# Differential attention scores: stacked rounded-precision matmuls on 128 rows for full-precision matmuls on 64 rows

## The chip, the cores and the metric

The kernel runs on one core of a Trainium2 chip. The metric is the device time of one execution in microseconds (us). The core's engines each run their own queue of instructions in order: PE (TensorE, matmuls), DVE (VectorE), ACT (ScalarE), POOL (GpSimd) and SP (SyncE, which here only issues DMAs). They wait for each other by semaphores.

## The reference, cut to what matters

The reference is a network of six layers on 512 tokens of width 1024: pooling, gated delta rule, latent attention (MLA), pooling, a state-space layer and, last, a layer of differential attention. Only the last one is touched. Cut to its core:

```python
def odd_layer(x, positions, ...):
    q, k, v, gate = jnp.split(rmsnorm_2(x, norm_w) @ w_in, 4, axis=-1)
    q = rmsnorm_2(q.reshape(bsz, s, 8, 2, 64), q_norm_w)   # 8 heads, 2 maps of width 64
    k = rmsnorm_2(k.reshape(bsz, s, 8, 2, 64), k_norm_w)
    q, k = partial_rotary(q, positions), partial_rotary(k, positions)
    # for each block of 128 queries:
    sc = jnp.einsum("bqhmd,bkhmd->bhmqk", qblk, k) * 64 ** -0.5
    pr = softmax(where(allowed, sc, -inf))                 # block-causal, chunks of 64
    wts = pr[:, :, 0] - lam * pr[:, :, 1]
    o = einsum("bhqk,bkhe->bqhe", wts, v)
    o = rmsnorm_2(o, subln_w) * (1 - lam_init)
    return x + (o.reshape(...) * silu(gate)) @ w_out
```

All data is float32.

## The kernel before

Activations lie transposed: a tile holds 128 channels on the partitions and 512 tokens. Most matmuls avoid full precision by splitting an operand into a rounded part and the rest. `split` makes the two with a cast on ACT (to the type fp32r) and a subtraction on DVE; `load_w` does the same for each slab of weights that a DMA on SP brings (L275 the load, L278 the cast, L279 the rest). `mm3` (L285 to L287) then adds three rounded matmuls: high by high, high by low, low by high.

The last layer is `odd`. For each of eight heads there is a unit for the query (`query`), one for the key (`key`), one for the gate, and one for v per two heads. Each is a projection of 24 rounded matmuls per 512 columns (`proj`). The query unit scales the result (L1407), squares it for its norm (L353) and rotates it (`rope`: L970 to L973, four DVE instructions). The key unit sums the squares with a full-precision matmul against a constant (L1398, called the norm matmul below), forms 1/sqrt on ACT by Ln and Exp (L371, L373), applies it (L1400) and rotates. Both end in one tile of 128 partitions: map 0 of the head on partitions 0 to 63, map 1 on 64 to 127. The tiles have the tag `t`, a pool of 8 buffers.

`attend` works on one head. For each block of 128 queries (`qb`, 0 to 3) and each of the two maps it forms the scores with one full-precision matmul on the map's 64 partitions (L1462), 128 to 512 columns wide, masks (L1463), and calls `softmax_rows` (L993 to L997: maximum on DVE, exponential on ACT, reciprocal). The two maps are combined (L1466, L1467). `weighted` transposes the result (L1007), copies it (L1009) and multiplies with v (L1011). Sums of the squares over the head (L365) give the last norm.

```python
rs = slice(m * 64, m * 64 + 64)
ps = self.ps("a")
nc.tensor.matmul(ps[:, :n], q[rs, sl], k[rs, :n], start=True, stop=True)
```

In the program, `attends` is a generator that the loop at the end of `odd` steps through between the units, by a table of numbers (`steps`); a head starts once its key is there. The final order of each engine's instructions is set when the kernel is built: a scheduler moves instructions within what data and buffers allow, so PE's queue mixes projections of later heads with the attention of earlier ones. The chip then runs each queue in that fixed order.

`stacked` exists already; the latent attention uses it for its rotated queries: of 64 partitions it makes a tile of 128, the rounded part on one half and the rest on the other.

Of the kernel before, what the change touches and what calls it, by code (L numbers as in the profile page):

```python
# [10 lines left out]
F32 = mybir.dt.float32  # L11
F32R = mybir.dt.float32r
I32 = mybir.dt.int32
AF = mybir.ActivationFunctionType
ALU = mybir.AluOpType
# [155 lines left out]
def step(chain, n):  # L171
    for _ in range(n):
        next(chain, 0)


def weave(units, *chains, drain=True):

    for u in units:
        u()
        for chain, n in chains:  # L180
            step(chain, n)
    if drain:
        for chain, _ in chains:
            for _ in chain:
                pass
# [7 lines left out]
class Net:  # L193
# [782 lines left out]
    def stacked(self, src, tag):  # L976
# [9 lines left out]
            out.append(t)  # L986
        return out

    def softmax_rows(self, ps, n, scale):

        nc = self.nc
        st = self.small([P, 4], "smx", 8)
        nc.vector.tensor_reduce(st[:, 0:1], ps[:, :n], axis=AX.X, op=ALU.max, negate=True)  # L993
        nc.vector.tensor_scalar(st[:, 1:2], st[:, 0:1], scale, None, op0=ALU.mult)  # L994
        pr = self.big("c")
        nc.scalar.activation(pr[:, :n], ps[:, :n], AF.Exp, bias=st[:, 1:2], scale=scale, accum_out=st[:, 2:3])  # L996
        nc.vector.reciprocal(st[:, 3:4], st[:, 2:3])  # L997
        return pr, st[:, 3:4]
# [373 lines left out]
    def odd(self):  # L1372
        nc, a = self.nc, self.a
        r = self.norm_r()
        rn = self.tok_r(r)
        cos, sin = self.rope_tables("pos2", "drope")
        mask = list(range(8, 16)) + list(range(8)) + list(range(16, 32))
        l4 = self.big("c", shape=[P, 4, 64])
        nc.gpsimd.dma_start(l4.rearrange("p a b -> p (a b)"), a["l4"].to_broadcast([P, 256]))
        pr = self.big("c", shape=[P, 2, 64])  # L1380
        lm = self.small([P, 4], "lam", 1)
        for i in range(2):
            nc.vector.tensor_tensor(pr[:, i], l4[:, 2 * i], l4[:, 2 * i + 1], op=ALU.mult)
            nc.vector.tensor_reduce(lm[:, i : i + 1], pr[:, i], axis=AX.X, op=ALU.add)
        nc.scalar.activation(lm[:, 0:2], lm[:, 0:2], AF.Exp)
        self.log_exp()
        nc.vector.tensor_tensor(lm[:, 2:3], lm[:, 1:2], lm[:, 0:1], op=ALU.subtract)
        nc.vector.tensor_scalar(lm[:, 2:3], lm[:, 2:3], -LAM_INIT, None, op0=ALU.add)
        nlam = lm[:, 2:3]

        def key(m):
            (ps,) = self.proj([a["dif_in"][m]], self.h, 8)
            st = sts[m - 8]
            st["qs"] = query_scale(st["q"][1])
            t = self.scaled(ps, r)
            (_, sq) = self.sq_add(None, t)
            p2 = self.ps("b")
            nc.tensor.matmul(p2, self.c("b64"), sq, start=True, stop=True)  # L1398
            rr = self.rsqrt(p2, 1.0 / 64, EPS, tag="t")
            nc.vector.scalar_tensor_tensor(t, t, self.p("kn"), rr, op0=ALU.mult, op1=ALU.mult)  # L1400
            return self.rope(t, cos, sin, mask, "t")

        def query(m):

            (ps,) = self.proj([a["dif_in"][m]], self.h, 8)
            t = self.big("t")
            nc.scalar.mul(t, ps, self.p("qn"))  # L1407
            (_, sq) = self.sq_add(None, ps)
            return self.rope(t, cos, sin, mask, "t"), sq

        def query_scale(sq):
            pn = self.ps("b")[:, :8].rearrange("p (c n) -> p c n", c=4)
            self.tok_sums(sq, self.c("b64")[:, 0:P:64], pn)
            return self.tok_scale(pn, rn, 64, 64.0**-0.5, "qs2", 2)

        y, sts = [], [{} for _ in range(8)]

        def v(hd):
            vN = [self.big("y", shape=[P, 2, 256]) for _ in range(2)]
            self.projn(  # L1420
                [a["dif_v"][hd + i] for i in range(2)], self.h, 4, 256,
                lambda t, ps: nc.scalar.mul(vN[t // 2][:, t % 2], ps, rn[:, t : t + 1]),
            )
            sts[hd]["v"] = sts[hd + 1]["v"] = vN

        def q(hd):
            sts[hd]["q"] = query(hd)

        def k(hd):
            sts[hd]["k"] = key(8 + hd)  # L1430

        def gate(hd):
            (ps,) = self.proj([a["dif_in"][16 + hd]], self.h, 8)
            sts[hd]["z"] = (self.scaled(ps, r, "y"), self.last, {})
            if hd % 2:
                self.silus([sts[i]["z"] for i in (hd - 1, hd)])
                for i in (hd - 1, hd):
                    sts[i]["g"] = sts[i]["z"][0]
                gated()

        def gated():

            while len(y) < 8 and "t" in sts[len(y)] and "g" in sts[len(y)]:
                t, g = sts[len(y)]["t"], sts[len(y)]["g"]
                nc.vector.tensor_tensor(t, t, g, op=ALU.mult)
                y.append(self.split(t))

        def attend(hd, st):
            vN = st["v"]
            q, qs, k = st["q"][0], st["qs"], st["k"]  # L1450
            po = self.ps("c")
            vs = slice((hd % 2) * P, (hd % 2) * P + P)
            vh = [vN[t // 2][:, t % 2, vs] for t in range(NC)]
            prev = None
            for qb in range(NC):
                n = (qb + 1) * P
                sl = slice(qb * P, n)
                pm = []
                for m in range(2):
                    rs = slice(m * 64, m * 64 + 64)  # L1460
                    ps = self.ps("a")
                    nc.tensor.matmul(ps[:, :n], q[rs, sl], k[rs, :n], start=True, stop=True)  # L1462
                    nc.vector.memset(ps[0:64, n - 64 : n], NEG)  # L1463
                    pm.append(self.softmax_rows(ps, n, qs[:, qb, m : m + 1]))
                (p0, r0), (p1, r1) = pm
                nc.vector.tensor_scalar(p1[:, :n], p1[:, :n], r1, nlam, op0=ALU.mult, op1=ALU.mult)  # L1466
                nc.vector.scalar_tensor_tensor(p0[:, :n], p0[:, :n], r0, p1[:, :n], op0=ALU.mult, op1=ALU.add)  # L1467
                if prev is not None:
                    self.weighted(*prev)
                prev = (p0, qb, vh, po, "y")  # L1470
                yield 1
            self.weighted(*prev)
            yield 1
            ro = self.rsqrt(self.sq_sum(self.sq_add(None, po), "b"), 1.0 / P, EPS, mul=1.0 - LAM_INIT)
            st["t"] = self.big("y")
            nc.vector.scalar_tensor_tensor(st["t"], po, self.p("subln"), ro, op0=ALU.mult, op1=ALU.mult)
            gated()
            yield 1

        def attends():  # L1480
            for hd in range(8):
                while "k" not in sts[hd]:
                    yield 1
                yield from attend(hd, sts[hd])

        chain = attends()
        order = [(u, 2 * p + i) for p in range(4) for u, i in ((v, 0), (q, 0), (k, 0), (q, 1), (k, 1), (gate, 0), (gate, 1))]
        order = order[:19] + order[21:26] + order[19:21] + order[26:]
        steps = (2, 2, 2, 0, 2, 1, 3, 2, 2, 3, 1, 3, 2, 1, 2, 2, 2, 1, 2, 2, 2, 2, 2, 2, 2, 3, 2, 2)
        for (u, hd), n in zip(order, steps):  # L1490
            u(hd)
            step(chain, n)
        last = [self.load_w(a["dif_out2"], D)]

        def slabs(m):
            return [(a["dif_out"][m], 7, 0, P), (last[0], 1, m * P, D)]

        early, rest = self.out_units(slabs, y, None, ["mm"] * 3)
        weave(early, (chain, 4))
        for u in rest:  # L1500
            u()
# [48 lines left out]
```

## Time and profile before

| | |
|---|---|
| median of 3 runs | 2570.8 us (2565.99 to 2572.75) |
| the profiled execution | 2575.46 us, its span 2573.7 us |
| mean granted clock of PE | 0.983 |
| PE busy | 2476.2 us (96%) |
| weight loads (PEld) | 1976.5 us (77%) |
| DVE busy | 1628.0 us (63%) |
| ACT busy | 1062.2 us (41%) |
| POOL busy | 466.2 us (18%) |

Busy times are sums over the whole span. PE's weight loads run beside its matmuls. Matmuls are pipelined: a listed duration overlaps the next one, so what a matmul costs is read from the distance between starts. The median and the profiled execution are different runs of the same kernel. POOL has no work in the last layer but two loads near its start.

### The profile page before, as it was taken

What the parts mean: (1) busy time and instruction counts of PE and PEld (TensorE: products, weight loads), DVE (VectorE), ACT (ScalarE), POOL (GpSimd) and SP (SyncE); (2) the same over time, 40 slices, a digit from 0 to 9 for tenths busy, and PEclk for the clock granted to TensorE, in tenths of its full rate; (3) what the DMA queues carried; (4) which work ended last, traced back from release to release, by engine and by line L of the source; (5) the groups of instructions that cost most, each with busy time, mean ns of one, the idle gap of its engine ahead of it and who ended that gap; (6) DMA issues with size and microseconds to landing.
All of it is one profiled execution on the core that took longest, in us unless ns stands there. A gap on an engine that the chain in (4) does not pass through costs nothing. (4 is left out here: it accounts for less than half of the span.)

```text
span 2573.7 us, 30632 instructions
## 1 busy us (share of the span) xinstructions
PE 2476.2 (96%) x11692; PEld 1976.5 (77%) x11692; DVE 1628.0 (63%) x2874; ACT 1062.2 (41%) x1676; POOL 466.2 (18%) x374
## 2 busy tenths in 40 slices
PE   8999999688899999999999999999999999999999
PEld 6888877476777888887787888887777767877877
DVE  6675368678556454355557366744997888477774
ACT  4333354134335343444445332333235546365553
POOL 0121103222321110000000112203334443200000
PEclk9999999799999999999999999999999999999999
DMA  4323224311211232211111233232222211321122
GB/s 152 98 91 99 94 82 127 100 36 46 80 56 58 90 95 97 86 60 56 62 58 53 95 98 95 94 100 88 83 88 67 67 50 58 113 66 58 58 64 76
DMA packets 81907, 205.63 MB, mean 80 GB/s; under 512 B 28352, under 2 KB 28480, under 8 KB 81760
## 3 DMA queue, kind: packets, MB, share of 16 engines
q1 hardware_dynamic: 81264, 202.23, 24.7%
q8 instruction: 92, 1.51, 0.2%
q0 software_dynamic: 208, 0.66, 0.1%
q10 hardware_dynamic: 288, 0.79, 0.1%
q14 instruction: 55, 0.45, 0.1%
HBM read 196.30 MB, written 7.34 MB: 79 GB/s over the span
## 5 line engine op out<-in xcount | busy, mean ns | idle before, releaser
L285 PE MATMUL psmm<-h,wh 128*128 128x512 f32 x1704 | 691.1, 406 | 47.9 <-DVE t L552 32.0
L278 ACT CAST wh<-wr 128x1024 fp32r<-128x1024 f32 (+3 forms) x366 | 376.6, 1030 | 779.2 <-PE psmm L286 591.5
L286 PE MATMUL psmm<-h,wh 128*128 128x512 f32 x1704 | 686.5, 403 | 0.1
L287 PE MATMUL psmm<-h,wl 128*128 128x512 f32 x1704 | 684.1, 401 | 0.0
L279 DVE TENSOR_TENSOR wl<-wr,wh 128x1024 fp32r<-128x1024 f32 (+2 forms) x270 | 322.1, 1193 | 185.9 <-ACT wh L278 182.4
L285 PEld LDWEIGHTS psmm<-h,wh 128*128 128x128 f32 x1704 | 324.9, 191 | 129.6 <-issue 54.5
L287 PEld LDWEIGHTS psmm<-h,wl 128*128 128x128 f32 x1704 | 324.3, 190 | 81.8 <-issue 14.7
L285 PE MATMUL psmm<-y,wh 128*128 128x512 f32 x976 | 385.2, 395 | 0.0
L286 PE MATMUL psmm<-y,wh 128*128 128x512 f32 x976 | 384.5, 394 | 0.0
L287 PE MATMUL psmm<-y,wl 128*128 128x512 f32 x976 | 383.0, 392 | 0.0
L286 PEld LDWEIGHTS psmm<-h,wh 128*128 128x128 f32 x1704 | 324.8, 191 | 73.3 <-issue 7.7
L279 POOL TENSOR_TENSOR wl<-wr,wh 128x1024 fp32r<-128x1024 f32 (+1 forms) x96 | 237.7, 2478 | 532.6 <-ACT wh L278 410.2
L351 POOL TENSOR_TENSOR sq<-sq,sq 128x512 f32<-128x512 f32 x36 | 64.5, 1791 | 845.4 <-ACT sq L353 845.4
L285 PEld LDWEIGHTS psmm<-y,wh 128*128 128x128 f32 x976 | 183.4, 188 | 38.9 <-issue 1.6
L286 PEld LDWEIGHTS psmm<-y,wh 128*128 128x128 f32 x976 | 183.5, 188 | 37.9 <-issue 2.2
L287 PEld LDWEIGHTS psmm<-y,wl 128*128 128x128 f32 x976 | 183.4, 188 | 37.5 <-issue 0.5
L1175 DVE SCALAR_TENSOR_TENSOR psa<-y,par,psa 128x506 f32<-128x506 f32 (+28 forms) x232 | 164.9, 733 | 3.2 <-ACT psa L1171 0.9
L480 DVE TENSOR_TENSOR x<-psmm,x 128x512 f32<-128x512 f32 x44 | 30.4, 692 | 140.2 <-PE psmm L287 140.2
L996 ACT ACTIVATE c<-psa,smx,qs 128x128 f32<-128x128 f32 (+3 forms) x128 | 78.8, 616 | 88.1 <-DVE smx L994 87.5
L492 DVE TENSOR_TENSOR t<-psmm,r 128x512 f32<-128x512 f32 (+1 forms) x74 | 50.9, 688 | 100.8 <-PE psmm L287 100.7
L552 DVE SCALAR_TENSOR_TENSOR t<-psmm,par,t 128x511 f32<-128x511 f32 (+2 forms) x120 | 89.0, 743 | 7.3 <-ACT t L547 5.4
L257 ACT CAST y<-c 128x512 fp32r<-128x512 f32 x60 | 37.1, 620 | 90.3 <-POOL c L528 69.3
(362 smaller groups left out, 3343.0 us busy)
## 6 DMA issues: line engine op xcount, KB each, us to landing
wr<-in_pool_in_dram SPq DMA_DIRECT2D x64, 512.0 KB, 3.4
wr<-in_gdn_in_dram SPq DMA_DIRECT2D x48, 512.0 KB, 3.5
wr<-in_ssd_in_dram SPq DMA_DIRECT2D x48, 512.0 KB, 3.4
wr<-in_pool_out_dram SPq DMA_DIRECT2D x32, 512.0 KB, 3.4
wr<-in_mla_in_dram SPq DMA_DIRECT2D x27, 512.0 KB, 3.4
wr<-in_dif_in_dram SPq DMA_DIRECT2D x24, 512.0 KB, 3.5
wr<-in_mla_uq_dram SPq DMA_DIRECT2D x24, 384.0 KB, 3.0
wr<-in_pool_grp_dram SPq DMA_DIRECT2D x16, 512.0 KB, 3.4
```

The costliest lines, as they stand in the source:

```text
L257: nc.scalar.copy(hi, src)
L278: nc.scalar.copy(hi[:, :f], raw[:, :f])
L279: self.rest.tensor_tensor(lo[:, :f], raw[:, :f], hi[:, :f].bitcast(F32), op=ALU.subtract)
L285: nc.tensor.matmul(ps, wh, xh, start=start, stop=False)
L286: nc.tensor.matmul(ps, wh, xl, start=False, stop=False)
L287: nc.tensor.matmul(ps, wl, xh, start=False, stop=stop)
L351: (eng or nc.gpsimd).tensor_tensor(acc[0], acc[0], acc[1], op=ALU.add)
L480: self.nc.vector.tensor_tensor(self.x[m], ps, self.x[m], op=ALU.add)
L492: self.last = self.nc.vector.tensor_tensor(t[:n], ps[:n], r[:n], op=ALU.mult)
L552: self.last = nc.vector.scalar_tensor_tensor(t[:, s:], u[:, : S - s], w(k), t[:, s:], op0=ALU.mult, op1=ALU.add)
L996: nc.scalar.activation(pr[:, :n], ps[:, :n], AF.Exp, bias=st[:, 1:2], scale=scale, accum_out=st[:, 2:3])
L1175: nc.vector.scalar_tensor_tensor(out[:, s:], z[:, : S - s], dw(k), acc[:, s:], op0=ALU.mult, op1=ALU.add)
```

## The change

The scores become two rounded matmuls over 128 partitions. With q = qh + ql and k = kh + kl (rounded part and rest), a tile with qh on one half of the partitions and ql on the other, times kh on both halves, gives (qh + ql) kh; times kl on both halves, (qh + ql) kl. So for each map the query is stacked (`stacked`, once per head for both maps: two tiles with tag `t` beside the rotated one), and the key becomes four tiles with tag `y` (36 buffers): for each map the rounded part and the rest, each on both halves. The new function `stacked_twice` writes the map's own half with a cast on ACT and a subtraction on DVE and copies it to the other half with a DMA from SBUF to SBUF, issued by POOL, 64 partitions x 512 words each.

```diff
+    def stacked_twice(self, src, tag):
+
+        nc = self.nc
+        out = []
+        for i in range(2):
+            a, b = slice(i * 64, i * 64 + 64), slice(64 - i * 64, 128 - i * 64)
+            hi, lo = self.big(tag, F32R), self.big(tag, F32R)
+            nc.scalar.copy(hi[a], src[a])
+            nc.vector.tensor_tensor(lo[a], src[a], hi[a].bitcast(F32), op=ALU.subtract)
+            nc.gpsimd.dma_start(hi[b], hi[a])
+            nc.gpsimd.dma_start(lo[b], lo[a])
+            out.append((hi, lo))
         return out
...
-            return self.rope(t, cos, sin, mask, "t")
+            return self.stacked_twice(self.rope(t, cos, sin, mask, "t"), "y")
...
-            return self.rope(t, cos, sin, mask, "t"), sq
+            return self.stacked(self.rope(t, cos, sin, mask, "t"), "t"), sq
...
-                    rs = slice(m * 64, m * 64 + 64)
                     ps = self.ps("a")
-                    nc.tensor.matmul(ps[:, :n], q[rs, sl], k[rs, :n], start=True, stop=True)
+                    hi, lo = k[m]
+                    nc.tensor.matmul(ps[:, :n], q[m][:, sl], hi[:, :n], start=True, stop=False)
+                    nc.tensor.matmul(ps[:, :n], q[m][:, sl], lo[:, :n], start=False, stop=True)
```

The existing function that the query now calls:

```python
def stacked(self, src, tag):
    for i in range(2):
        a, b = slice(i * 64, i * 64 + 64), slice(64 - i * 64, 128 - i * 64)
        t = self.big(tag, F32R)
        nc.scalar.copy(t[a], src[a])
        nc.vector.tensor_tensor(t[b], src[a], t[a].bitcast(F32), op=ALU.subtract)
        out.append(t)
```

Lines after `stacked` stand 14 or 15 higher in the changed kernel (L1462 becomes L1476 and L1477, L1007 is L1021, L1011 is L1025, L1398 is L1412). The scheduler sets a new order in the whole layer. Three places follow, each before and then after.

PE at the first scores of the sixth head, before: the two maps' scores of the first block (psa) stand next to each other behind a sum of squares (L365).

```order
L285 MATMUL psmm_18607<-wh_18552,h_16738 128x256
L286 MATMUL psmm_18607<-wl_18553,h_16738 128x256
L287 MATMUL psmm_18607<-wh_18552,h_16739 128x256
L365 MATMUL psb_18660<-sq_18658,ones 128x512
L1462 MATMUL psa_18668<-t_18497,t_18406 128x128
L1462 MATMUL psa_18677<-t_18497,t_18406 128x128
L285 MATMUL psmm_18694<-h_16443,wh_18690 128x512
```

The same place after, from the last projection matmuls of the unit ahead of it; y_18636 and y_18637 are the first map's key (rounded part, rest), y_18642 and y_18643 the second's.

```order
L285 MATMUL psmm_18844<-h_16738,wh_18840 128x512
L286 MATMUL psmm_18844<-h_16739,wh_18840 128x512
L287 MATMUL psmm_18844<-h_16738,wl_18841 128x512
L1476 MATMUL psa_18816<-y_18636,t_18537 128x128
L1025 MATMUL psc_18446<-y_18674,y_18182 128x128 x2
L1025 MATMUL psc_18446<-y_18674,y_18183 128x128
L1021 MATMUL psb_18679<-con,c_18655 128x128 x4
L1477 MATMUL psa_18816<-y_18637,t_18537 128x128
L1476 MATMUL psa_18826<-y_18642,t_18540 128x128
L1477 MATMUL psa_18826<-y_18643,t_18540 128x128
```

Where two matmuls stood there are four, with other work between them. The norm matmul of this head's key stands 21 projection matmuls of 512 columns and three transposes ahead of the first one.

PE in the third head from the 512 column scores on, before: projection matmuls (psmm) stand between scores and transposes (L1007).

```order
L286 MATMUL psmm_17929<-h_16632,wh_17925 128x512
L1462 MATMUL psa_17789<-t_17670,t_17581 128x512
L1011 MATMUL psc_17675<-y_17744,y_17373 128x128 x2
L1462 MATMUL psa_17798<-t_17670,t_17581 128x512
L287 MATMUL psmm_17929<-h_16631,wl_17926 128x512
L285 MATMUL psmm_17929<-h_16669,wh_17925 128x512
L286 MATMUL psmm_17929<-h_16670,wh_17925 128x512
L287 MATMUL psmm_17929<-h_16669,wl_17926 128x512
L285 MATMUL psmm_17929<-h_16738,wh_17925 128x512
L286 MATMUL psmm_17929<-h_16739,wh_17925 128x512
L1007 MATMUL psb_17809<-con,c_17727 128x128 x3
```

The same head after, from its last 384 column scores to their transposes (L1021, x3).

```order
L1476 MATMUL psa_17805<-y_17739,t_17641 128x384
L1477 MATMUL psa_17805<-y_17740,t_17641 128x384
L1476 MATMUL psa_17871<-y_17733,t_17638 128x512
L1021 MATMUL psb_17817<-con,c_17775 128x128 x2
L1477 MATMUL psa_17871<-y_17734,t_17638 128x512
L1025 MATMUL psc_17745<-y_17820,y_17421 128x128 x2
L1476 MATMUL psa_17881<-y_17739,t_17641 128x512
L1477 MATMUL psa_17881<-y_17740,t_17641 128x512
L1021 MATMUL psb_17893<-con,c_17802 128x128 x3
```

No projection matmul stands there any more; between the scores and their transposes there are only this head's own matmuls.

POOL at the start of the last layer, before: its two loads of positions and constants are its last work.

```order
L351 TENSOR_TENSOR sq_16447<-sq_16447,sq_16598 128x512
L351 TENSOR_TENSOR sq_16447<-sq_16447,sq_16636 128x512
L351 TENSOR_TENSOR sq_16447<-sq_16447,sq_16674 128x512
L946 DMA c_16764<-in_pos_dram 128x512
L1379 DMA c_16791<-in_l_dram 128x256
```

After: behind them stand the copies of the key tiles, here those of the first head and the first two of the second.

```order
L946 DMA c_16764<-in_pos_dram 128x512
L1393 DMA c_16791<-in_l_dram 128x256
L998 DMA y_17030<-y_17030 64x512
L998 DMA y_17036<-y_17036 64x512
L999 DMA y_17031<-y_17031 64x512
L999 DMA y_17037<-y_17037 64x512
L998 DMA y_17203<-y_17203 64x512
L998 DMA y_17209<-y_17209 64x512
```

There are 32 of them, four for each head, on a queue that was empty.

## Rows read from the trace of the kernel before

**Rows 1.** Windows: length, busy PE, PEld, DVE, ACT, POOL, granted clock, DMA

```profile
2260.00:2540.00 280.00, 275.87 (x1385) 205.19 (x1384) 202.83 (x573) 160.54 (x307) 0.00 (x0) 0.99 0.20 62
2420.00:2440.00 20.00, 20.00 (x123) 15.35 (x122) 18.41 (x64) 11.09 (x26) 0.00 (x0) 1.00 0.16 54
```

**Rows 2.** The chain of waits from 2260 us on, by line

```profile
by line: PE psmm L287 22.5%; PE psmm L285 22.1%; PE psmm L286 22.1%; PE psa L1462 11.5%; PE psc L1011 6.6%; PE psb L1007 3.1%; PE psb L1398 2.3%; PE psb L365 2.2%; PE psb L414 2.0%; issue 0.7%; ACT t L371 0.4%; ACT L428 0.4%; ACT L373 0.4%;
```

**Rows 3.** PE's timeline: start, us, line, operation, out<-in, passes

```profile
2357.55 0.40 PE L287 MATMUL psmm<-h,wl 128*128 128x512 f32 x1
2357.79 0.39 PE L285 MATMUL psmm<-h,wh 128*128 128x512 f32 x1
2358.11 0.70 PE L1462 MATMUL psa<-t,t 64*128 64x256 f32 x4
2358.74 0.50 PE L286 MATMUL psmm<-h,wh 128*128 128x512 f32 x1
...
2366.98 1.12 PE L1462 MATMUL psa<-t,t 64*128 64x512 f32 x2
2368.04 0.50 PE L287 MATMUL psmm<-h,wl 128*128 128x512 f32 x1
2368.38 0.39 PE L285 MATMUL psmm<-h,wh 128*128 128x512 f32 x1
...
2383.73 0.28 PE L287 MATMUL psmm<-wh,h 128*128 128x256 f32 x1
2383.85 0.28 PE L285 MATMUL psmm<-wh,h 128*128 128x256 f32 x1
```

**Rows 4.** PE's timeline, the first and the last group of score matmuls

```profile
2281.58 0.49 PE L1462 MATMUL psa<-t,t 64*128 64x128 f32 x4 [1.05 <-DVE t L973]
...
2521.04 1.12 PE L1462 MATMUL psa<-t,t 64*128 64x512 f32 x2
```

**Rows 5.** Groups by line in the MLA layer: busy us, mean ns, idle before

```profile
L984 ACT CAST h<-t 64x512 fp32r<-64x512 f32 x16 | 9.9, 619 | 14.4 <-DVE t L973 14.2
...
L985 DVE TENSOR_TENSOR h<-t,h 64x512 fp32r<-64x512 f32 x16 | 11.0, 686 | 2.5 <-ACT h L984 2.1
```

**Rows 6.** Timelines of PE, ACT and DVE on the way of two keys

```profile
2273.11 1.02 PE L1398 MATMUL psb<-sq,con 128*128 128x512 f32 x2
...
2291.37 1.28 ACT L373 ACT_TABLE_LOAD   x1
...
2415.83 1.02 PE L1398 MATMUL psb<-sq,con 128*128 128x512 f32 x2
...
2421.01 0.69 DVE L973 TENSOR_TENSOR t<-t,c 128x512 f32<-128x512 f32 x1
...
2421.78 0.49 PE L1462 MATMUL psa<-t,t 64*128 64x128 f32 x4
```

**Rows 7.** DMA issues: queue, count, KB each, median us to landing

```profile
y<-d SPq DMA_DIRECT2D x32, 32.0 KB, 2.0
...
c<-in_pos_dram POOLq DMA_DIRECT2D x2, 256.0 KB, 3.1
...
c<-in_l_dram POOLq DMA_DIRECT2D x1, 128.0 KB, 3.6
```

**Rows 8.** Groups by line and form from 2240 us on: softmax at 384 columns

```profile
L993 DVE TENSOR_REDUCE smx<-psa 128x1 f32<-128x384 f32 x16 | 8.8, 552 | 0.2
...
L996 ACT ACTIVATE c<-psa,smx,qs 128x384 f32<-128x384 f32 x16 | 10.8, 673 | 11.8 <-DVE smx L994 11.8
...
L1466 DVE TENSOR_SCALAR c<-c,smx,lam 128x384 f32<-128x384 f32 x8 | 3.7, 458 | 0.1
L1467 DVE SCALAR_TENSOR_TENSOR c<-c,smx,c 128x384 f32<-128x384 f32 x8 | 4.9, 607 | 0.1
```

**Rows 9.** PE's timeline at an idle time, and the window behind it

```profile
2296.65 1.17 PE L1011 MATMUL psc<-y,y 128*128 128x128 f32 x4 [2.91 <-ACT y L1009]
...
2298.00:2300.00 2.00, 2.00 (x6) 1.57 (x5) 1.88 (x6) 0.44 (x1) 0.00 (x0) 0.50 0.00 0
```

More of the change, by code (lines that the diff above doesn't have):

```diff
@@ L987, in stacked @@
         return out
+    def stacked_twice(self, src, tag):
[9 more added lines that the diff above has]
+            out.append((hi, lo))
+        return out
     def softmax_rows(self, ps, n, scale):
```

## The prediction

> **What bounds the kernel now.** I read the windows of the last layer first, then the chain of waits there, then PE's timeline. The last layer, with the differential attention, runs from about 2260 us to the end. In 2260 to 2540 PE shows work for 275.87 of 280 us, DVE for 202.83, ACT for 160.54 [rows 1]. PE is the bound, with DVE at 72% behind it. The chain of waits agrees: nearly all of it is PE, and the score matmuls (L1462) hold 11.5% of the 313.7 us from 2260 to the end of the span [rows 2], that is 36.1 us. The other five layers are not touched, so the answer lies in this stretch.
>
> **What leaves PE.** Each full-precision score matmul is two passes (the timeline counts 2 for one instruction). In [rows 3] compare the starts: a score of 512 columns starts at 2366.98 and lets the next instruction in at 2368.04, 1.06 us for one; a rounded matmul of 512 columns lets the next in after 0.24 (2357.55 to 2357.79), and I take 0.23; one of 256 columns after 0.12 (2383.73 to 2383.85). The pair of 256 columns (x4) starts at 2358.11 and is done at 2358.74, 0.63 for both, so the two halves of 64 rows ran beside each other. There is also a price at the edges: 0.32 from 2357.79 to the score instead of 0.23, and 0.34 after it (2368.04 to 2368.38). That is 0.09 + 0.11 = 0.20 for each group of scores that stands between other matmuls; I counted 46 groups from the first at 2281.58 to the last at 2521.04 [rows 4], 9.2 us.
>
> The Trainium skill (TensorEngine Tiling (Array Packing), Key Properties) says that a change of tiling mode drains the engine; the trace agrees with these 0.2 us. The same section says that different tiles work in parallel, which speaks against the change: if every pair ran as the 256 pair did, the scores would have cost about half as much, and some 10 us would be saved instead of 25 (an estimate). By the trace it is mostly the 128 and 256 pairs that stand back to back.
>
> Before: 36.1 + 9.2 = 45.3. After: 128 rounded matmuls, 32 of each width. With 0.23 and 0.12 from rows, 0.18 for 384 (between them) and 0.10 for 128 (an estimate below the 0.12, since a weight load stands beside each): 32 x 0.63 = 20.2. **PE loses 25.1 us.** If the edges stay it is 16; much above 26 it cannot be.
>
> **What DVE and ACT get.** Each head adds 4 casts on ACT and 4 subtractions on DVE of 64x512. The MLA layer has both: 619 ns and 686 ns [rows 5]. 32 of each: ACT +19.8, DVE +22.0. Over 280 - 25 = 255 us DVE would be at 224.8, 88%. The stretch 2420 to 2440 held 18.41 of 20 with PE full [rows 1], so 88% can be covered, but with little slack; its cost shows as lateness, below.
>
> **The longer way of k.** This is the wait that the change adds. In the fifth head the norm matmul of k starts at 2415.83, the last step of the rotation starts at 2421.01 and takes 0.69, and the first score follows at 2421.78: 5.95 in all, PE just in time [rows 6]. Now the first half needs one cast (0.62) and a DMA before its first matmul, the last one a cast, two subtractions (1.37) and a DMA. The DMA is issued by POOL, SBUF to SBUF, 128 KB; the trace has none such. Nearest are POOL's own loads: 3.6 us for 128 KB and 3.1 for 256 KB; the least is 2.0 on SP for 32 KB [rows 7]. I take 3.1 and keep 2.0 and 3.6. Four stand behind each other on POOL's queue; the subtractions that feed them come 0.69 apart, so the queue itself adds little. Need from norm matmul to score: 5.95 + 0.62 + 3.1 = 9.7 for the first, 5.95 + 0.62 + 1.37 + 3.1 = 11.0 for the last of the four.
>
> What PE has to do meanwhile I counted in the new order with the intervals above (estimates: the norm matmul 0.87, two passes as in the 1.06 row without the edges; a transpose 0.12; a product with v 0.21). For the sixth head: 0.87 + 21 x 0.23 + 3 x 0.12 = 6.0 to the first score, 7.0 to the last. For heads one to eight, to first / last: 10.1/12.3, 7.9/9.1, 10.8/12.8, 6.8/7.8, 10.8/13.1, 6.0/7.0, 10.4/12.8, 14.6/16.2. Four heads fall short: the second by 2.0, the fourth by 3.3, the sixth by 4.1, and the first. There the way took 8.47 (2273.11 to 2281.58, PE idle for 1.05), and the new order of ACT has one table load more on it (1.28): 8.47 + 1.28 + 0.62 + 3.1 = 13.5 against 10.1, 3.4 [rows 4, 6]. Behind a waiting score on PE stand the projections of the next units, so the wait is whole. **Sum 12.8 us**; 8.4 with 2.0, 14.8 with 3.6.
>
> **The softmax with less cover.** In the third head PE now runs out of projections: between the last 384 score and its transposes stand 1.6 us of PE work. Four of the steps between take 552 + 673 + 458 + 607 ns = 2.29 [rows 8], so at least 0.7 is idle. I counted five or six such places, among them the products with v that now follow their copy closely. I take 6 us, 2 to 10, with the fuller DVE in it. Gone or contained are the two idle times that PE has today, 1.05 [rows 4] and 2.91 [rows 9]: -4.0.
>
> **The clock.** After today's 2.91 us of idle PE the next 2 us ran at a granted 0.50, the lower level (1.2 GHz) [rows 9]; with what lies beside it, about 1.5 us lost. Three of the new waits are longer than 2.91, one such place goes: +3.0.
>
> **Sum:** -25.1 + 12.8 + 6 - 4 + 3 = **-7.3 us**. The profiled execution took 2575.5 (span 2573.7 and 1.8 around it), so 2568.2 for it; it was 4.7 above the median of the three runs, 2570.8, so 2563.5 there.
>
> **Rivals.**
> *The cover holds.* The copies land in about 2 us, the DVE runs its steps closer than their durations, and the waits overlap (PE waiting for k lets DVE catch up with the softmax). Then 25.1 stands against some 5 to 8: -18, 2553. For it: PE was never idle at the softmax today. Against it: four heads fall short even at 2.0.
>
> *The copies come late, and it is slower.* The place is POOL's queue, the price a wait of PE at every head. Each us over 3.1 costs 4 us in the four short heads, and from 4.2 on the third, fifth and seventh wait too. At 6 us: 6.3 + 4.9 + 1.8 + 6.1 + 1.8 + 6.9 + 2.2 = 30 us, and four clock drops less one (4.5): -25.1 + 30 + 6 - 4 + 4.5 = +11, 2582. The saving is gone from about 4.4 us a copy, and the kernel is slower by over 0.3% from about 5.4. For it: four copies at once and DVE at 88%. Against it: no POOL load took over 3.6.
>
> The Trainium skill (SBUF — State Buffer, "SBUF: two separate sides") has a rule for this: a DMA issued by POOL waits for its descriptors while DVE runs an operation in the mode that takes both ports, of which it names the fp32 copy. No run here shows it yet; by that rule the copies would be late whenever such an operation stands beside them.
>
> *PE gains less than it seems.* The weight loads of the 128-column matmuls don't hide, and the edges of 0.2 stay, since the transposes around the scores are full precision too: 16 instead of 25, so +2, 2573, no change.
>
> **How the numbers follow.** The forecast (2557 to 2571 by its own bounds) has 0.5, the cover 0.2, late copies 0.2, the small gain 0.1. A measurement of this kernel can tell about 0.3%, 7.7 us, from no change. Half of the forecast lies beyond that and with the cover makes 0.44 faster; the other half with most of the small gain and a part of the late copies 0.36 the same; 0.20 slower. The range leaves out the ends of the cover and of the late copies: 2548 to 2582.
>
> **What would show it.** Right: the score matmuls' share of the chain falls to about 20 us; 32 issues on POOL's queue that land in about 3 us; PE idle before the first scores of the second, fourth and sixth heads, 2 to 4 us each, with the granted clock low behind it; DVE near 225 us in a stretch some 7 us shorter. Wrong: copies that land well under 2 or over 5 us; PE without waits at k; PE idle mostly on the weights' second halves (L279), which would mean that DVE is the bound; or intervals above 0.3 us at the new 512-column scores.

## The result, and the profile after

The changed kernel takes 2607.3 us (median of 4 runs, 2600.8 to 2613.2) against 2570.8 before: 1.0144 times as long, 95% interval 1.0111 to 1.0177. Forecast were 2563.5 us and a range of 2548 to 2582. It is slower by 36.5 us where a small gain was forecast.

The profiled execution has a span of 2611.4 us, 37.7 more than before. All of it lies in the last layer, whose first projection matmul starts at 2258.58 us (before: 2258.53). The four executions had spans of 2599.1 to 2611.4 us at mean granted clocks of 0.981 to 0.976; the profiled one is the longest, so what it loses to the clock below is at the upper end. The window that answers to [rows 1] shows PE busy for 249.91 of 280 us at a mean granted clock of 0.92; before it was 275.87 at 0.99. DVE and ACT do not rise in it (200.41 and 158.62), since it holds less of a layer that got longer; over the whole span DVE rose from 1628.0 to 1648.1 us and ACT from 1062.2 to 1084.6, near the forecast (22.0 and 19.8):

```profile
2260.00:2540.00 280.00, 249.91 (x1254) 204.41 (x1253) 200.41 (x546) 158.62 (x300) 16.57 (x32) 0.92 0.26 73
```

PE's four largest waits in the last layer (what waited, for what; us in total, times, longest). Before there were two in all, 2.9 and 1.1 us:

```profile
PE psa L1476 <- DMA y<-y: 14.4, 6, 6.6
PE psmm L285 <- DVE t L492: 5.2, 2, 4.4
PE psa L1476 <- ACT c L1010: 4.4, 6, 1.1
PE psb L1021 <- DVE c L1482: 3.8, 3, 1.7
```

The score matmuls do nearly what the sum said. In PE's timeline of the changed kernel a score matmul of 512 columns starts at 2341.53 and lets the next in after 0.23, one of 256 columns after 0.17 and 0.12; next to a projection the edges of [rows 3] (0.32 ahead, 0.34 behind) are 0.23:

```profile
2341.53 0.40 PE L1477 MATMUL psa<-y,t 128*128 128x512 f32 x1
2341.76 0.39 PE L285 MATMUL psmm<-h,wh 128*128 128x512 f32 x1
2341.99 0.39 PE L286 MATMUL psmm<-h,wh 128*128 128x512 f32 x1
...
2342.67 0.39 PE L286 MATMUL psmm<-h,wh 128*128 128x512 f32 x1
2342.90 0.39 PE L1476 MATMUL psa<-y,t 128*128 128x512 f32 x1
...
2372.33 0.33 PE L1476 MATMUL psa<-y,t 128*128 128x256 f32 x1
2372.50 0.28 PE L1477 MATMUL psa<-y,t 128*128 128x256 f32 x1
2372.62 0.40 PE L286 MATMUL psmm<-h,wh 128*128 128x512 f32 x1
```

Over the whole layer they take longer: where PE does not wait and has the upper clock, the distances to the next start average 0.16, 0.14, 0.22 and 0.27 us for 128, 256, 384 and 512 columns, some 25 us for the 128 matmuls where the sum had 20.2.

To see where the time went I cut the last layer, from 2260 us to 14 us before the end, into windows of 2 us. In each, idle is its length less PE's busy time, and the loss to the clock is PE's busy time times (1 - granted clock). What is left of the time from 2260 us to the end, the "rest", is PE's work at full clock (with the last 14 us whole). It is rough, since a PE shown as busy may still wait: e12 below has the same matmuls as before, and a rest 5.7 us longer.

| | idle | clock | rest | together |
|---|---|---|---|---|
| before | 4.1 | 1.5 | 308.0 | 313.7 |
| after | 37.6 | 21.7 | 292.1 | 351.4 |
| difference | +33.5 | +20.2 | -15.9 | +37.7 |

So PE has less work, and loses more than three times as much to waits and to the lower clock. The rows on the way of the sixth head's key, in order of start, show such a wait: the norm matmul (L1412) at 2466.38, PE's last projection at 2472.64, the last step of the rotation at 2472.66 (DVE), the first cast at 2473.54 (ACT), the four copies issued from 2474.44 to 2476.98 (POOL), and the score at 2479.60. PE was idle for 6.57 us. (Rows by engine, PE first.)

```profile
2466.38 1.50 PE L1412 MATMUL psb<-sq,con 128*128 128x512 f32 x2
...
2472.64 0.39 PE L287 MATMUL psmm<-h,wl 128*128 128x512 f32 x1
2479.60 0.44 PE L1476 MATMUL psa<-y,t 128*128 128x128 f32 x1 [6.57 <-DMA y<-y]
...
2472.66 0.68 DVE L973 TENSOR_TENSOR t<-t,c 128x512 f32<-128x512 f32 x1
...
2473.54 0.61 ACT L996 CAST y<-t 64x512 fp32r<-64x512 f32 x1
...
2474.44 0.51 POOL L998 DMA_DIRECT2D y<-y  x1 [27.62 <-ACT y L996]
...
2476.98 0.51 POOL L999 DMA_DIRECT2D y<-y  x1 [0.36 <-issue]
```

The copies, by group (KB each, median us to landing), and the least, median and longest of half of them:

```profile
y<-y POOLq DMA_DIRECT2D x32, 128.0 KB, 2.7
```

```profile
DMA to landing us min/median/max: 2.1/2.7/5.0
```

The median hides what PE waited for. Of the five longest pieces in the chain of waits from 2260 us on, three are copies (start, length):

```profile
2286.64 3.99 DMA y<-y
...
2444.89 4.99 DMA y<-y
2474.44 5.02 DMA y<-y
```

PE's waits that end with these three are 4.08, 1.92 and 6.57 us, 12.6 of the 15.0 that it waits for copies (14.4 and 0.6, L1476 and L1477). Beside each of them runs a load of weights, issued by SP; for the last one:

```profile
2474.54 0.33 SPq L275 DMA_DIRECT2D wr<-in_dif_in_dram  x1
```

By the landing times in the trace, the 12 copies with no such load in flight beside them landed in 2.1 to 2.6 us, the other 20 in 2.2 to 5.0, thirteen of these in 3.8 or more. The ten kernels with such copies agree: of the 162 copies with no load beside them all but one (3.7) landed in 2.1 to 3.1 us, of the 126 others the longest took 6.0. No run moved the loads, so it is likely, and not shown, that they make the copies late.

The subtractions take what those of [rows 5] took:

```profile
L985 DVE TENSOR_TENSOR t<-t,t 64x512 fp32r<-64x512 f32 x16 | 11.0, 686 | 0.9 <-ACT t L984 0.4
L997 DVE TENSOR_TENSOR y<-t,y 64x512 fp32r<-64x512 f32 x16 | 10.9, 684 | 1.0 <-ACT y L996 0.7
```

And the granted clock (third value from the end) stays at the lower level for 12 us in this stretch; in the first 8 PE waits now and then, in the last 4 it does not:

```profile
2380.00:2384.00 4.00, 2.77 (x9) 1.54 (x7) 3.23 (x9) 1.26 (x4) 0.00 (x0) 0.50 0.18 69
2384.00:2388.00 4.00, 3.14 (x14) 3.06 (x15) 3.89 (x12) 2.52 (x5) 0.00 (x0) 0.50 0.00 0
2388.00:2392.00 4.00, 4.00 (x15) 2.86 (x14) 2.17 (x10) 1.13 (x6) 0.00 (x0) 0.50 0.00 0
2392.00:2396.00 4.00, 4.00 (x35) 4.00 (x34) 2.64 (x5) 1.25 (x2) 0.00 (x0) 0.97 0.00 0
```

### The profile page after: what moved, and what is told of

Its sections match the earlier page's. It is cut to its first block, busy times and chain, and to the rows that moved or that the text cites. A ratio compares the mean times of both kernels' runs of the same rounds, so it can differ in the third digit from the quotient of the medians.

```text
span 2611.4 us, 30803 instructions
## 1 busy us (share of the span) xinstructions
PE 2478.7 (95%) x11692; PEld 1996.5 (76%) x11692; DVE 1648.1 (63%) x2906; ACT 1084.6 (42%) x1710; POOL 484.1 (19%) x406
## 5 line engine op out<-in xcount | busy, mean ns | idle before, releaser
L480 DVE TENSOR_TENSOR x<-psmm,x 128x512 f32<-128x512 f32 x44 | 30.3, 691 | 139.2 <-PE psmm L287 139.2
L492 DVE TENSOR_TENSOR t<-psmm,r 128x512 f32<-128x512 f32 (+1 forms) x74 | 50.8, 687 | 96.6 <-PE psmm L287 96.4
L257 ACT CAST y<-c 128x512 fp32r<-128x512 f32 x60 | 37.1, 620 | 90.4 <-POOL c L528 69.3
```

The lines of the kernel that those rows point to most:

```text
L257: nc.scalar.copy(hi, src)
L480: self.nc.vector.tensor_tensor(self.x[m], ps, self.x[m], op=ALU.add)
L492: self.last = self.nc.vector.tensor_tensor(t[:n], ps[:n], r[:n], op=ALU.mult)
```

## The experiments

Two theories stood first. Theory 1: the change makes the key's way from norm matmul to score longer, PE waits there and then runs at the lower clock. Theory 2: DVE and ACT are too full with the added casts and subtractions. A third came up later: what PE saves in this layer turns into waits by itself. All ratios are to the kernel before as it ran beside the other, with 95% intervals; its median lay between 2570.8 and 2576.5 us there, so the ratios compare better than the times. The split into idle, clock and rest is made as above from one profile each. In these profiles the layer starts between 9.2 us earlier and 5.7 later than before, because the layers ahead of it took less or more time; the rest is corrected by that.

| | time us | ratio | idle | clock | rest |
|---|---|---|---|---|---|
| before | 2570.8 | 1 | 4.1 | 1.5 | 308.0 |
| after | 2607.3 | 1.0144 (1.0111 to 1.0177) | 37.6 | 21.7 | 292.1 |
| e1_engines | 2604.8 | 1.0109 (1.0077 to 1.0141) | 30.3 | 17.6 | 291.7 |
| e3_split64 | 2595.6 | 1.0074 (1.0046 to 1.0102) | 10.6 | 11.6 | 313.7 |
| e4_before_copy | 2615.6 | 1.0155 (1.0125 to 1.0186) | 11.8 | 22.0 | 317.3 |
| e8_key_first | 2586.9 | 1.0044 (1.0029 to 1.0060) | 22.6 | 6.2 | 292.9 |
| e14_swap | 2580.6 | 1.0026 (1.0011 to 1.0041) | 20.8 | 10.5 | 290.2 |
| e12_before_key_first | 2576.6 | 1.0005 (0.9994 to 1.0016) | 4.3 | 0.0 | 313.7 |
| e10_keys_two | 2586.4 | 1.0038 (1.0023 to 1.0053) | 19.3 | 15.7 | 289.3 |
| e17_split64_key_first | 2598.1 | 1.0090 (1.0068 to 1.0112) | 11.5 | 9.3 | 317.3 |
| e18_swap_pool | 2584.4 | 1.0044 (1.0027 to 1.0061) | 23.7 | 12.2 | 289.8 |
| e19_swap_steps | 2593.5 | 1.0076 (1.0059 to 1.0093) | 26.8 | 15.7 | 290.4 |
| e22_one_rounded | 2577.8 | 1.0017 (1.0008 to 1.0027) | 14.1 | 8.9 | 294.3 |
| e23_copy_key_first | 2578.4 | 1.0019 (1.0007 to 1.0031) | 3.7 | 0.0 | 314.7 |
| e24_key_first_gates | 2583.1 | 1.0029 (1.0014 to 1.0043) | 21.5 | 3.5 | 291.8 |
| e25_one_rounded_kf_gates | 2569.8 | 0.9982 (0.9969 to 0.9996) | 11.2 | 4.4 | 295.0 |
| e26_before_kf_gates | 2583.0 | 1.0029 (1.0012 to 1.0046) | 5.8 | 6.4 | 312.0 |
| e27_swap_gates | 2579.0 | 1.0014 (0.9999 to 1.0028) | 19.8 | 9.0 | 290.3 |

### The copy by itself: e4, e23 and their control e12

e4 adds to the kernel before only a copy of the rotated key:

```diff
-            return self.rope(t, cos, sin, mask, "t")
+            t = self.rope(t, cos, sin, mask, "t")
+            kc = self.big("y")
+            for i in range(2):
+                nc.gpsimd.dma_start(kc[i * 64 : i * 64 + 64], t[i * 64 : i * 64 + 64])
+            return kc
```

> The kernel before, with the rotated key of each head copied once from SBUF to SBUF by two DMAs on POOL's queue before the scores read it; full-precision scores on 64 rows as before, no added cast or subtraction. Theory 1: the copy alone costs 10 us or more, 2580 to 2600. Theory 2: PE finds other work, within 4 us of 2571.

Measured 2615.6, beyond theory 1's range: the copy alone, with no cast, no subtraction and no gain, costs as much as the whole change. Theory 2 cannot give that. Idle rose by only 7.7 us, with 5.7 us of waits for the copy; 20.5 are clock and 9.3 lie in the rest. For the clock, PE's timeline around the third head: some 2.5 us after 1.73 us of waiting for the copy the clock falls, the projection matmuls start 0.43 apart instead of 0.23, and do so still at 2395, though PE does not wait again:

```profile
2372.06 0.49 PE L1466 MATMUL psa<-y,t 64*128 64x128 f32 x2 [1.73 <-DMA y<-t]
...
2377.27 0.63 PE L287 MATMUL psmm<-h,wl 128*128 128x512 f32 x1
2377.70 0.63 PE L285 MATMUL psmm<-h,wh 128*128 128x512 f32 x1
...
2395.54 0.63 PE L285 MATMUL psmm<-h,wh 128*128 128x512 f32 x1
2395.97 0.63 PE L286 MATMUL psmm<-h,wh 128*128 128x512 f32 x1
```

The windows beside it: PE busy for all of the 4 us, and the granted clock at 0.50, its lower level (1.2 GHz):

```profile
2376.00:2380.00 4.00, 4.00 (x8) 1.69 (x7) 0.90 (x5) 0.70 (x3) 0.00 (x0) 0.50 0.00 0
2380.00:2384.00 4.00, 4.00 (x10) 2.15 (x9) 1.92 (x7) 1.71 (x3) 0.00 (x0) 0.50 0.00 0
2384.00:2388.00 4.00, 4.00 (x9) 2.04 (x8) 1.86 (x4) 0.37 (x1) 0.00 (x0) 0.50 0.21 60
2388.00:2392.00 4.00, 4.00 (x11) 2.68 (x11) 3.47 (x11) 1.63 (x4) 0.00 (x0) 0.50 0.18 71
2392.00:2396.00 4.00, 4.00 (x8) 2.01 (x8) 0.49 (x3) 0.00 (x0) 0.00 (x0) 0.50 0.02 4
```

Part of the rest is the pairs. One score of 256 columns alone takes PE as long as the pair of [rows 3], 0.63 us; before, in the second head:

```profile
2321.20 0.70 PE L1462 MATMUL psa<-t,t 64*128 64x256 f32 x2
2321.83 0.39 PE L287 MATMUL psmm<-wh,h 128*128 128x256 f32 x1
```

Before, 7 of the 9 groups of 128-column scores and 6 of 10 of 256 hold both maps (x4); here none of 16 and 2 of 14 do. In the order set for two halves of a key that are copied one behind the other, the two maps' scores mostly stand apart, with projections between them. At 0.42 us for each of 7 more groups of 128 and 0.63 for each of 4 of 256 that is 5.5 of the 9.3 us (an estimate).

The key unit ahead of the query unit gives the copy 24 more projection matmuls of cover. The edit for e8, e12, e17 and e23:

```diff
-            st["qs"] = query_scale(st["q"][1])
...
             sts[hd]["q"] = query(hd)
+            sts[hd]["qs"] = query_scale(sts[hd]["q"][1])
...
-                while "k" not in sts[hd]:
+                while "k" not in sts[hd] or "q" not in sts[hd]:
...
-((v, 0), (q, 0), (k, 0), (q, 1), (k, 1), (gate, 0), (gate, 1))
+((v, 0), (k, 0), (q, 0), (k, 1), (q, 1), (gate, 0), (gate, 1))
```

> The kernel before with the key copied by two DMAs (which cost 40 us) and the key unit ahead of the query unit, a unit of cover for the copy. Theory 1: the copy is covered and its cost goes nearly whole: 2572 to 2585. Rival (the DMAs cost wherever they lie, by the port or the queue): over 2600.

> The kernel before with each head's key unit ahead of its query unit: the control for the new unit order, full-precision scores on 64 rows. Theory 1: there PE had next to no waits at the key, so the order alone gives nothing: 2567 to 2578. If it gains 8 us or more, what the changed kernel regained by that order was the order's own.

With cover the same copy costs 0.19% instead of 1.55%; the same order without the copy costs nothing (1.0005). The 16 DMAs cost little in themselves, though three of them landed late here too (3.6 to 4.6 us). Busy time and clock of e23 in the window of [rows 1], as before the change:

```profile
2260.00:2540.00 280.00, 276.27 (x1364) 202.00 (x1364) 197.76 (x565) 159.38 (x303) 8.25 (x16) 1.00 0.23 68
```

### The changed kernel with more cover: e8, e10, e14, e1

> The changed kernel with each head's key unit ahead of its query unit (24 projection matmuls of 512 columns, 5.5 us, more between the key's norm matmul and the first score; the query's shorter way comes last). Theory 1: most waits of PE for the copies go, 2580 to 2590. Theory 2: DVE and ACT have the same work, within 6 us of 2607.

2586.9, as theory 1 had it; by the ratios that is some 26 of the 37 us. The layer is 29.6 us shorter than in the profile of the change: 15.0 are idle time, as much as PE waited for the copies, and 15.5 the clock (the profile of the change is of its longest execution). No wait for a DMA is left; the largest that are left are waits for the softmax and at the layer's output (L257):

```profile
PE psa L1475 <- ACT c L1010: 7.6, 6, 2.6
PE psmm L285 <- ACT y L257: 3.4, 2, 2.1
PE psb L1021 <- DVE c L1481: 2.6, 2, 1.7
```

e10 puts both keys ahead of both queries, `((v, 0), (k, 0), (k, 1), (q, 0), (q, 1), ...)`:

> The changed kernel with both keys of a pair of heads ahead of both queries. The first key has two units of cover, but the first head's scores wait for its query. Theory 1: waits for the copies all gone; 2575 to 2590, if the later query does not become the next wait.

2586.4, by the ratio no more than e8 gained.

e14 swaps the roles, so that the copies lie on the query's way:

```diff
-    return self.stacked_twice(self.rope(t, cos, sin, mask, "t"), "y")
+    return self.stacked(self.rope(t, cos, sin, mask, "t"), "t")
...
-    return self.stacked(self.rope(t, cos, sin, mask, "t"), "t"), sq
+    return self.stacked_twice(self.rope(t, cos, sin, mask, "t"), "y"), sq
...
-    hi, lo = k[m]
+    hi, lo = q[m]
     nc.tensor.matmul(ps[:, :n], hi[:, sl], k[m][:, :n], start=True, stop=False)
     nc.tensor.matmul(ps[:, :n], lo[:, sl], k[m][:, :n], start=False, stop=True)
```

> The changed kernel with the roles swapped: the query is written as four tiles with the 32 DMAs, the key is stacked once without a DMA. The same number of casts, subtractions, DMAs and score matmuls; only the way on which the DMAs lie is another (the query is ready a unit earlier, 5.5 us of PE work). Theory 1 (what lengthens the key's way costs, nothing else): the 2.7 us of the DMA leave the key's way but 1.3 us of cast and subtraction stay: 2580 to 2592, below the 2607 of the changed kernel. Theory 2 (fuller DVE and ACT): within 6 us of 2607.

2580.6, with the same casts, subtractions, DMAs and matmuls as the change. By the ratios some 30 of its 37 us hang on the way on which the copies lie. Again no DMA is among the waits:

```profile
PE psc L1025 <- ACT y L1023: 7.1, 4, 5.2
PE psa L1476 <- DVE t L985: 3.2, 2, 2.0
PE psb L1021 <- DVE c L1482: 3.0, 2, 1.7
```

e1 writes the second halves with ACT and DVE (`nc.scalar.copy(hi[b], src[a])` and the same subtraction into `lo[b]`) instead of the DMAs:

> The second halves of the key tiles are written by ACT (cast) and DVE (subtraction) instead of the 32 DMAs: no copies, but ACT gets about 20 us and DVE 22 us more than in the changed kernel. If the late copies are the cause (theory 1: PE waits for them, then runs at the lower clock), the way of the key is shorter by about 2.7 - 1.3 = 1.4 us per half and the time falls to about 2585 to 2595 (changed kernel 2607). If the fuller DVE and ACT are the cause (theory 2), it rises to 2615 or more.

2604.8, neither: 10 us above theory 1's range and not slower as theory 2 had it. The key's way is shorter (in the sixth head 7.99 us from the norm matmul to the first score, in the change 13.22), and PE waits 6.5 us for the key's halves (4.6 for ACT's casts, 1.9 for DVE's subtractions) instead of 15.0. But the other waits stay at some 24 us, and 17.6 are lost to the clock. ACT and DVE got 8 and 12 us more busy time than in the change (1092.9 and 1659.9 us), not the 20 and 22 of the expectation, since 16 casts and 16 subtractions were added.

### Other attempts: e3, e17, e18, e19

e3 splits query and key once and uses `mm3` on 64 rows, without copies: `self.split(self.rope(...), "y")` and `"t"`, and `self.mm3(ps[:, :n], (q[0][rs, sl], q[1][rs, sl]), (k[0][rs, :n], k[1][rs, :n]), True, True)`. e17 is e3 with the key first.

> From the kernel before: query and key are split once (one cast and one subtraction of 128x512 each, both maps together), and the scores are three rounded matmuls on 64 rows (rounded by rounded, rounded by rest, rest by rounded). No copies, half the added work on ACT and DVE (about +10 and +11 us), PE at 3 passes instead of 4 halves. Theory 1 (copies): no wait for a DMA is left, so the PE saving shows: 2550 to 2565, faster than before. Theory 2 (DVE and ACT): half of the loss stays, 2575 to 2590.

> Three rounded matmuls on 64 rows (key and query split once, no copies) with the key unit ahead of the query unit. Theory 1: its loss of 0.7% came from the key's way being longer by a cast and a subtraction, 1.3 us, so it goes: 2568 to 2578, the same as before, since its PE work was no smaller. Theory 2: within 5 us of 2593.

2595.6 and 2598.1, where theory 1 had a gain for e3 and no change for e17: both expectations failed. PE's rest is 313.7 and 317.3, not below the 308.0 of before, so three passes on 64 rows save nothing, and e3 says nothing on the copies. The key first did not help, so that e3's loss came from the key's way is not borne out either.

e18 moves the query's subtraction in e14 from DVE to POOL (`nc.gpsimd.tensor_tensor(lo[a], ...)` behind the first copy):

> The swapped kernel (query as four tiles with DMAs, key stacked) with the query's two subtractions on POOL, which has no other work but the DMAs there: 16 subtractions, 11 us, leave DVE; the key's way is not touched, the query's gets longer by about 2 x 1.1 us but has a unit of cover. Theory 1 (only the length of a way without cover costs): the same as the swapped kernel, 2575 to 2585. Theory 2 (fuller DVE): it gains, 2560 to 2573.

2584.4, in theory 1's range and no gain. The test is weaker than meant: DVE's busy time over the span fell from 1647.7 to 1643.3 us, by 4.4 instead of 11. Against theory 2 e4, e8 and e14 count for more.

e19 raises entries of the steps table in e14 (from the 22nd on: 2, 2, 2, 2, 3, 2, 2 becomes 3, 2, 3, 3, 3, 3, 3):

> The swapped kernel with five of the last seven entries of the steps table raised by one, so that the last heads' attention is asked for earlier and has projections beside it. In the swapped kernel PE is idle for about 7 us between 2500 and 2540, after the last projections. Theory 1: these waits are from lack of cover, so some 3 to 6 us are regained: 2572 to 2578. If the scheduler's order hangs on other things, no change, 2580.

2593.5, 13 us slower than e14, which neither expectation had. The scheduler answers with another order of the whole layer, and that is worth as much as the effects sought.

### Does PE's saving show at all? e22, and e24 to e27

e22 takes the PE work away and adds nothing: the rotation's last addition writes the rounded type, and a score is one rounded matmul on 64 rows.

```diff
-        nc.vector.tensor_tensor(t, t, sh, op=ALU.add)
-        return t
+        o = self.big("y", dt) if dt else t
+        nc.vector.tensor_tensor(o, t, sh, op=ALU.add)
+        return o
```

> The kernel before with the last addition of the rotation writing the rounded type, and the scores as one rounded matmul on 64 rows: the rests of query and key are left out. No instruction is added, no way gets longer; PE has one pass instead of two slower ones, at least as much off as in the change (25 us or more). Theory 1 (the change loses by the key's way): the saving shows, 2540 to 2555. Rival (whatever PE saves in this layer comes back as waits for the softmax and as lower clock): 2560 to 2572.

2577.8, not faster but 0.17% slower than before. The rival is right in kind, and the time is even above its range. PE's rest falls by 13.7, idle rises by 10.0 and the clock's loss by 7.4. Window and waits of e22:

```profile
2260.00:2540.00 280.00, 265.93 (x1306) 203.62 (x1305) 198.15 (x568) 157.99 (x306) 0.00 (x0) 0.96 0.19 60
```

```profile
PE psa L1463 <- ACT c L997: 5.8, 6, 1.9
PE psmm L285 <- ACT y L257: 2.1, 1, 2.1
PE psa L1463 <- DVE y L974: 1.8, 2, 1.1
PE psb L1008 <- DVE c L1468: 1.7, 1, 1.7
```

The waits are spread over the softmax (L997 the exponential, L1468 the combining of the maps) and the end of the layer (L257, the split of the last outputs). Its timeline puts 7 of the 14 us between 2500 and 2540, where the last heads run with no projection beside them. The next four move the second pair's gate units behind the last pair's query and key units, for more projections there:

```diff
-order = order[:19] + order[21:26] + order[19:21] + order[26:]
+order = order[:12] + order[14:19] + order[21:26] + order[12:14] + order[19:21] + order[26:]
```

> The changed kernel with the key unit first and the two gate units of the second pair moved behind the last pair's query and key units: 2 x 5.5 us more projections beside the last heads' attention. If the saving of PE is lost because PE has no other work beside the attention there (theory 3), the waits between 2500 and 2540 go and with them the lower clock: 2565 to 2577, from 2583. If not, 2580 to 2590.

> One rounded matmul per score on 64 rows (rests left out), key unit first, the second pair's gate units moved behind: no added instruction, less PE work, more cover. Theory 3: now the saving shows, 2552 to 2568. Otherwise as without the new order, 2573 to 2580.

> Control: the kernel before with the key unit first and the same gate units moved. Theory 3: it has no waits to lose there (4 us of idle PE in the layer), so 2568 to 2578, no change.

> The swapped kernel (copies on the query's way) with the same gate units moved. Theory 3: 2560 to 2572, from 2580; otherwise 2577 to 2590.

Theory 3, in the narrow form that the end of the layer is the place, does not hold: e24 and e27 gain some 0.15 and 0.12% on e8 and e14, within their intervals, and their idle time stays at about 20 us. In place of several waits at the last head PE now waits once for 5.6 us at the layer's output (L257), in e25 too. e25 gains 0.35% on e22 and is the only kernel below before (0.9982), and it leaves the rests out. Its control e26 lost 0.29%, against the expectation of no change, so in this order one rounded matmul is worth 0.47%, 12 us. PE's saving shows in one order and not in another. The stacked scores cost nothing in this order, but gain nothing either: e24 and e26 are both at 1.0029, with 20.2 us less of PE's work in e24's profile than in e26's, and 15.7 us more of idle time.

## Why the prediction was wrong

**PE's saving.** Next to projections the count was right: 0.23 and 0.12 per matmul and no edges. In sum it was somewhat low, some 25 us for the score matmuls where 20.2 were entered. The step that failed is to enter the saving at full size, -25.1, with PE as the bound. The layer is a chain as well: projections, norm, rotation, softmax and products, each handed over between PE, ACT and DVE, in an order laid for the longer PE work. The rest fell by 16 (by 20.8 and 20.2 in two other orders, e8 against e12 and e24 against e26), and e22 shows that such a saving by itself comes back as waits and clock.

**The longer way of k.** Right in kind, and near in sum, 12.8 us forecast and 15.0 measured, but in part by luck. The first and sixth head waited 4.1 and 6.6 (3.4 and 4.1 forecast), the second and fourth hardly (2.0 and 3.3 forecast), since PE had waited elsewhere in the meantime, and the fifth 1.9 where nothing was forecast. And a copy did not take 3.1 us, but 2.1 to 2.6 where no load of weights ran beside it and up to 5.0 otherwise; the long waits stand at late ones. The rival of late copies is wrong by its condition: it needs over 5.4 us for every copy, the longest took 5.0, and the result is beyond its 2582. Its mechanism, a wait of PE for a late copy, is there in three heads, without the reason that it gave (four copies at once and a full DVE). The Trainium skill's rule (SBUF — State Buffer, "SBUF: two separate sides"), by which a DMA issued by POOL waits while DVE runs an operation that takes both ports, is shown by no run: four copies issued between DVE's subtractions (2318.12 to 2320.66) landed in 2.2 to 2.6 us.

**The softmax with less cover.** Forecast +6 - 4 = +2, measured 33.5 - 15.0 = +18.5 of other idle time. This and the clock are the terms that were too small. The -4 was wrong in kind, too: the wait of 2.91 in [rows 9] did not go. Two table loads of ACT for the query's scale (L427, L428) had held up the copy (L1009) for which PE waited there; now they hold up DVE, which empties a projection's buffer (L492) only after the scale, and PE waits 4.39 for that buffer:

```profile
2305.32 1.28 ACT L428 ACT_TABLE_LOAD   x1
...
2306.86 0.17 DVE L396 TENSOR_TENSOR qs2v<-qs2v,qs 128x8 f32<-128x8 f32 x1 [1.23 <-ACT qs L428]
...
2307.68 0.58 PE L285 MATMUL psmm<-wh,h 128*128 128x256 f32 x1 [4.39 <-DVE t L492]
```

In all 5.8 us of PE's waits are for DVE at L492, a wait for which the sum had no term.

**The clock.** Forecast +3, measured +20.2. I priced a drop by the one in [rows 9], some 3 us at the lower level; here 12 us and in e4 some 20 followed waits. With e8, half of what the cover gave back was clock. What keeps the clock at the lower level for so long is not shown by any run.

**DVE.** 88% on average was no obstacle in itself: e4 has no added DVE work and is as slow, e14 has all of it and loses 0.26%.

So -25.1, +12.8, +2 and +3 were -15.9, +15.0, +18.5 and +20.2: +37.8 instead of -7.3. Open is why about 20 us of idle PE or more stay in every version with the stacked scores, wherever the copies and gates lie; two changes of order did not remove them, and I have no run that names one cause.

## What to carry to other kernels

Where an engine is busy all the time because a laid-out order feeds it, its saved work is not yet saved time: first try the saving alone, with nothing added (e22 is an edit of a few lines), and see whether it shows. A copy of 2 to 5 us costs next to nothing or 40 us depending on the way on which it lies, so put it on the operand that is ready earlier. Where PE waits for a DMA, read the landing of that very DMA and what ran beside it, not the median of the group. Price a wait on PE with the clock behind it, and read how long that lasts from more than one place.

## What the runs showed of the hardware

The lower clock outlasts the wait ahead of it: in e4 a wait of 1.73 us was followed by some 20 us at a granted 0.50 with PE busy throughout, before by about 3 us after 2.91 of idle. A DMA of 128 KB from SBUF to SBUF on POOL's queue landed in 2.1 to 3.1 us where no load of weights was in flight beside it (161 of 162 in ten kernels), and in up to 6.0 where one was; POOL issues one in 0.51. Two full-precision matmuls on the two halves of the rows that stand next to each other in PE's queue run beside each other: 0.63 us for a pair of 256 columns, and 0.63 for one alone.
